# Feed-forward blocks: hidden-state tiles moved by 128 bytes in their partition

## The chip, the cores and the metric

One Trainium2 chip, one of its cores. The metric is the device time of one execution in microseconds, lower is better.

## The reference, cut to what matters

Two decoder layers over 512 tokens of width 1024, in float32. Each layer runs a SwiGLU feed-forward block, a token mixer (differential attention in layer 0, a pooling mixer in layer 1), cross-attention into 256 memory tokens, and a second feed-forward block; a layer norm follows each. The change touches the four feed-forward blocks:

```python
def swiglu_ffn(x, w_in, w_out):          # w_in: 1024 x 5632, w_out: 2816 x 1024
    h = x @ w_in
    g, u = jnp.split(h, 2, axis=-1)
    return (jax.nn.silu(g) * u) @ w_out
```

## The kernel before, in words

**Precision.** A float32 operand is split into a high part, rounded to the matmul engine's float32r type, and the remainder. `split` makes both, the high part on ScalarE (ACT), the low one on VectorE (DVE). `mm3` (lines 231 to 233) multiplies with three matmuls: high by high, high by low, low by high. In `mm3(out, w, x)` w is the stationary operand, loaded 128 columns at a time, and x the moving one, streamed through.

**A feed-forward block** (`ffn`) cuts the 2816 hidden units into eleven columns of 256.
- `up` computes one column: seven products of blocks of x and of w_in (a scheme of seven products in place of eight), each of 24 matmuls with 256 moving columns, summed in PSUM tiles named x, y and z. The weights (wh, wl) are stationary, x is moving: from xh and xl, or from sums of its blocks in xe. The first product of a column that goes by passes is recorded at line 773.
- `seven` forms the blocks and sums of h that the second matrix product needs, and splits them into the tiles ha and hb.
- `down` multiplies two columns of h by their rows of w_out, again in seven products, each of 12 matmuls with 512 moving columns, into px, py and pz. Here h (ha, hb) is stationary and the weights (wh, wl) are moving. DVE adds each result into the tokens X.
- `plain_down` does the last three columns without that scheme, into ps; there h stands in xe. For the first half of the output columns the weights stand in wh and wl, for the second half in hb and ha (line 983 on).

The order is written out by hand (`FFN_TURNS`): in the first turn three columns of `up` alone, then four turns in which products of two columns of `up` alternate with the products of one `down`, and `plain_down` at the end. One product of `up` or two (24 or 48 matmuls) stand between two blocks of `down`.

**Queues.** Weights come by DMA from the SP and POOL queues into ra, rc (for w_in) and b1 to b4 (for w_out), and are split into wh and wl just ahead of their product.

**Where the tiles lie.** A pool is a run of bytes in every partition; pools stack up in the order in which they are entered. `stage_pools` makes wh, wl, ra, rc, `phase_pool` the rest in the order of its arguments. Pads set the addresses modulo 512 bytes: `to_w` ahead of wh (64 bytes in this stage), and `to_x` (448 bytes) where a phase names `_x`. All tiles of the stage are whole multiples of 512 bytes. So, counted from the end of the tiles xh and xl, the weights stand at 64 modulo 512, and xe, hb, sp, ha, sr and hr at 0:

```python
APART, ROUND, LINE = {"ffn": 64, "da": 448, "pool": 64}, 512, 480
...
    def to_x(self, ctx):

        self.pad(ctx, ROUND - self.apart)
```

The pooling mixer and the cross-attention of layer 1 use the same 64 bytes; there the query projection (output xq) has the weights (wh, wl) stationary and xh, xl moving, with 512 columns.

Of the kernel before, what the change touches and what calls it, by code (L numbers as in the profile page):

```python
# [126 lines left out]
class Trunk:  # L127
# [49 lines left out]
    @contextmanager  # L177
    def phase_pool(self, gain, spare, **bufs):

        self.gain, self.spare, self.bufs, self.phase = gain, spare, bufs, {}
        with ExitStack() as ctx:
            for t in bufs:
                if t == "_x":
                    self.to_x(ctx)
                elif t == "_w":
                    self.to_w(ctx)
                else:
                    self.phase[t] = self.stage.get(t) or ctx.enter_context(self.pool(t))  # L190
            yield
# [1540 lines left out]
        return self.stage_pools(5, dict(raw=raw), order)  # L1732

    def ffn_phase(self, **more):
        bufs = dict(b1=1, b3=1, b2=1, b4=1, _x=0, xe=6, hb=4, sp=4, ha=4, sr=1, hr=3)
        return self.phase_pool(("hr", "sr"), "sp", **bufs, **more)

    def ffn_first(self, layer, ln):
# [84 lines left out]
```

## Time and profile before

| | |
|---|---|
| median of 3 runs | 1897.52 us (1895.87 to 1897.72) |
| profiled execution | 1899.25 us, its span 1897.5 us |
| granted TensorE clock | 0.999 |
| TensorE matmul busy | 1886.5 us (99%), 13120 matmuls |
| TensorE weight load busy | 1730.9 us (91%) |
| VectorE, ScalarE, GpSimd busy | 1540.9, 1000.8, 308.2 us |
| HBM read | 274.79 MB |

In rows of the profile PE is TensorE's matmul, PEld its weight load, DVE VectorE, ACT ScalarE, POOL GpSimd; L232 is line 232 of the kernel. A row of a group ends with its busy time, the mean duration in ns of one instruction, and the idle time ahead of them. A matmul's duration (some 0.28 us with 256 columns, 0.39 with 512) is longer than the distance from its start to the next one's, since matmuls are pipelined: how fast they follow each other is read from start times. In a row of the timeline the first number is the start and the second the duration in us, and of a tile's names the one ahead of the arrow is written. In a row of the chain the second number is the time that the instructions named there take on it.

### The profile page before, as it was taken

Reading aid. Unit: us, or ns where it says so; the run is one execution under the profiler, and the core shown is the slowest. Engines: PE = TensorE matmul, PEld = TensorE weight load, DVE = VectorE, ACT = ScalarE, POOL = GpSimd, SP = SyncE. Lnnn points to the kernel's source line nnn. Section 1 sums busy time; section 2 is a strip of 40 time slices with the busy share of each in tenths; the row PEclk is TensorE's granted clock in tenths of the full one; section 3 lists DMA queues with packets and bytes.
Section 4 is the critical chain, followed back from the end, with each engine's and each line's share of the span. In section 5 each row is a group of like instructions: output and inputs, shape, how many; then the busy total and the mean of one; then the engine's idle time right before and its main releaser. Section 6 shows DMA issues by size and latency. Waiting matters only on the chain.

```text
span 1897.5 us, 32589 instructions
## 1 busy us (share of the span) xinstructions
PE 1886.5 (99%) x13120; PEld 1730.9 (91%) x13120; DVE 1540.9 (81%) x2246; ACT 1000.8 (53%) x1542; POOL 308.2 (16%) x274
## 2 busy tenths in 40 slices
PE   9999999999999999999999999999999999999998
PEld 8999998888889988999998999999899889999996
DVE  7888989888876558889887988898786568998886
ACT  6555554566654435555554655555455436555552
POOL 3112120112110002221220311212120012211210
PEclk9999999999999999999999999999999999999999
DMA  9978772322235327987785687777464438867861
GB/s 254 215 178 178 171 141 85 103 69 75 91 112 178 112 70 181 195 177 168 144 188 168 118 179 181 168 166 162 157 172 146 142 69 180 173 159 178 185 129 53
DMA packets 250055, 283.20 MB, mean 149 GB/s; under 512 B 8752, under 2 KB 213040, under 8 KB 249904
## 3 DMA queue, kind: packets, MB, share of 16 engines
q0 software_dynamic: 94080, 94.38, 32.3%
q1 hardware_dynamic: 155824, 186.74, 30.2%
q8 instruction: 103, 1.69, 0.4%
q14 instruction: 48, 0.39, 0.1%
HBM read 274.79 MB, written 4.19 MB: 147 GB/s over the span
## 4 chain that ended last, share of the span: by engine, by line
PE 96%; DMA 2%; DVE 1%; ACT 0%; SPq 0%; issue 0%; POOL 0%; DVEq 0%; ACTq 0%
PE x L231 7%; PE x L232 7%; PE x L233 7%; PE ps L231 5%; PE ps L233 4%; PE ps L232 4%; PE z L231 4%; PE z L233 4%; PE z L232 4%; PE px L233 3%; PE px L231 3%; PE px L232 3%; PE x L773 3%; PE y L231 2%; PE y L232 2%; PE y L233 2%
## 5 line engine op out<-in xcount | busy, mean ns | idle before, releaser
L741 POOL DMA_DIRECT2D ra<-in_ffn_w_in_dram x132 | 170.7, 1307 | 977.6 <-DVE wl L748 960.4
L746 ACT CAST wh<-ra 128x1024 fp32r<-128x1024 f32 x176 | 184.9, 1053 | 197.8 <-PE x L232 63.8
L748 DVE TENSOR_TENSOR wl<-ra,wh 128x1024 fp32r<-128x1024 f32 x176 | 214.2, 1220 | 64.7 <-ACT wh L746 64.0
L231 PE MATMUL x<-xe,wh 128*128 128x256 f32 x704 | 195.0, 277 | 0.0
L232 PE MATMUL x<-xe,wh 128*128 128x256 f32 x704 | 194.8, 277 | 0.0
L233 PE MATMUL x<-xe,wl 128*128 128x256 f32 x704 | 194.8, 277 | 0.0
L746 ACT CAST wh<-rc 128x1024 fp32r<-128x1024 f32 x132 | 138.9, 1053 | 100.3 <-PE x L232 41.6
L143 ACT CAST wh<-b 128x1024 fp32r<-128x1024 f32 x112 | 117.8, 1052 | 134.8 <-PE x L232 62.2
L748 DVE TENSOR_TENSOR wl<-rc,wh 128x1024 fp32r<-128x1024 f32 x132 | 159.5, 1218 | 24.7 <-ACT wh L746 24.7
L144 DVE TENSOR_TENSOR wl<-b,wh 128x1024 fp32r<-128x1024 f32 x112 | 136.7, 1220 | 40.9 <-ACT wh L143 40.9
L231 PE MATMUL x<-xh,wh 128*128 128x256 f32 x536 | 148.7, 277 | 0.0
L232 PE MATMUL x<-xl,wh 128*128 128x256 f32 x536 | 148.4, 277 | 0.0
L233 PE MATMUL x<-xh,wl 128*128 128x256 f32 x536 | 148.4, 277 | 0.0
L231 PEld LDWEIGHTS x<-xe,wh 128*128 128x128 f32 x704 | 132.4, 188 | 1.3
L232 PEld LDWEIGHTS x<-xe,wh 128*128 128x128 f32 x704 | 132.3, 188 | 1.3
L233 PEld LDWEIGHTS x<-xe,wl 128*128 128x128 f32 x704 | 132.2, 188 | 0.0
L144 DVE TENSOR_TENSOR wl<-raw,wh 128x1024 fp32r<-128x1024 f32 x64 | 78.5, 1233 | 45.8 <-ACT wh L143 45.2
L231 PEld LDWEIGHTS x<-xh,wh 128*128 128x128 f32 x536 | 100.8, 188 | 0.7
L232 PEld LDWEIGHTS x<-xl,wh 128*128 128x128 f32 x536 | 100.8, 188 | 0.7
L233 PEld LDWEIGHTS x<-xh,wl 128*128 128x128 f32 x536 | 100.7, 188 | 0.0
L143 ACT CAST wh<-raw 128x1024 fp32r<-128x1024 f32 x64 | 66.4, 1049 | 62.5 <-PE xq L232 18.2
L231 PE MATMUL z<-xe,wh 128*128 128x256 f32 x352 | 97.5, 277 | 0.0
(445 smaller groups left out, 6239.9 us busy)
## 6 DMA issues: line engine op xcount, KB each, us to landing
ra<-in_ffn_w_in_dram POOLq DMA_DIRECT2D x132, 512.0 KB, 7.0
rc<-in_ffn_w_in_dram SPq DMA_DIRECT2D x88, 512.0 KB, 5.8
b<-in_ffn_w_out_dram SPq DMA_DIRECT2D x76, 512.0 KB, 5.0
ra<-in_ffn_w_in_dram SPq DMA_DIRECT2D x44, 512.0 KB, 4.7
rc<-in_ffn_w_in_dram POOLq DMA_DIRECT2D x44, 512.0 KB, 7.3
raw<-in_xa_wkv_dram SPq DMA_DIRECT2D x16, 1024.0 KB, 5.4
raw<-in_da_w_qkv_dram SPq DMA_DIRECT2D x24, 512.0 KB, 3.7
raw<-in_xa_wq_dram SPq DMA_DIRECT2D x8, 1024.0 KB, 5.2
```

Of the source, the lines that this page charges most:

```text
L143: self.nc.scalar.copy(hi, src),
L144: self.nc.vector.tensor_sub(lo, src, hi.bitcast(F32)),
L231: self.first_mm = mm(out, w[0], x[0], start=start, stop=False, skip_group_check=again)
L232: mm(out, w[0], x[1], start=False, stop=False, skip_group_check=again)
L233: self.last_mm = mm(out, w[1], x[0], start=False, stop=stop, skip_group_check=again)
L741: nc.gpsimd.dma_start(t, source(*block), accum_op=ALU.add)
L746: hi = nc.scalar.copy(v[0], raw)
L748: lo = nc.vector.tensor_sub(v[1], raw, v[0].bitcast(F32))
L773: self.last_mm = nc.tensor.matmul(ps[:, j], v[i][:, k, j * P : (j + 1) * P], x[l][:, k], start=n == i == l == 0, stop=n == 7 and i == 1, s ...
```

## The change

A pad of 128 bytes (twice 64) is entered between xe and hb. hb, sp, ha, sr and hr of the feed-forward blocks move up by 128 bytes: ha and hb stand at 128 modulo 512, 64 above the weights, where they stood at 0, 64 below. Nothing else is added or moved: the instructions and their order are the same.

```diff
@@ phase_pool @@
                 elif t == "_w":
                     self.to_w(ctx)
+                elif t == "_h":
+                    self.pad(ctx, 2 * self.apart)
                 else:
@@ ffn_phase @@
-        bufs = dict(b1=1, b3=1, b2=1, b4=1, _x=0, xe=6, hb=4, sp=4, ha=4, sr=1, hr=3)
+        bufs = dict(b1=1, b3=1, b2=1, b4=1, _x=0, xe=6, _h=0, hb=4, sp=4, ha=4, sr=1, hr=3)
```

## The prediction

> **What bounds the kernel now.** I read the page first: the share of each engine, the clock, and the chain that ended last. Then what the matmul engine waited for, and last the start times of matmuls, which say what the page's means can't.
>
> ```profile
> span 1897.5 us, 32589 instructions
> PE 1886.5 (99%) x13120; PEld 1730.9 (91%) x13120; DVE 1540.9 (81%) x2246; ACT 1000.8 (53%) x1542; POOL 308.2 (16%) x274
> PEclk9999999999999999999999999999999999999999
> PE 96%; DMA 2%; DVE 1%; ACT 0%; SPq 0%; issue 0%; POOL 0%; DVEq 0%; ACTq 0%
> ```
>
> The matmul engine is busy 99% of the span at the full granted clock in all 40 slices, and 96% of the chain is its own work. Its waits, in total:
>
> ```profile
> PE idle L138 <- DVE hb L595: 1.3, 1, 1.3
> PE ps L231 <- DVE X L380: 0.8, 1, 0.8
> PE y L773 <- ACT wh L746: 0.5, 1, 0.5
> ```
>
> The longest are 1.3, 0.8 and 0.5 us. So nothing that happens on another engine or in a transfer is worth anything here. What counts is how fast matmuls of one shape follow each other, and the change touches just that: the address of an operand.
>
> Define the offset of a matmul as the address of its stationary operand less that of its moving one, modulo 512 bytes. All tiles of the feed-forward stage are whole multiples of 512 bytes and all slices start on such multiples, so only the pads count: x (xh, xl, xe) stands at 0, the weights (wh, wl) at 64, and ha, hb at 0 now. In `up` weights are stationary and x moves: +64. In `down` h is stationary and weights move: -64. In the second half of `plain_down` h from xe is stationary and weights in hb and ha move: 0; in its first half weights in wh move: -64. In layer 1's cross-attention the query projection has weights at 64 stationary and x at 0 moving, 512 columns wide: +64, the offset that `down` is to get.
>
> Matmul starts from the timeline of TensorE, first row of a block and first row of what follows:
>
> ```profile
> 816.02 0.39 PE L231 MATMUL pz<-wh,hb 128*128 128x512 f32 x1
> ...
> 818.77 0.28 PE L231 MATMUL z<-xe,wh 128*128 128x256 f32 x1
> ```
>
> `down` (-64): 12 matmuls in 2.75 us, 229.2 ns each.
>
> ```profile
> 1451.86 0.39 PE L231 MATMUL xq<-xh,wh 128*128 128x512 f32 x1
> ...
> 1454.66 0.28 PE L231 MATMUL xs<-kv,q 128*128 128x256 f32 x1
> ```
>
> The query projection (+64): 12 in 2.80 us, 233.3 ns each.
>
> ```profile
> 1035.26 0.39 PE L231 MATMUL ps<-ha,xe 128*128 128x512 f32 x1
> ...
> 1040.70 0.40 PE L231 MATMUL ps<-wh,xe 128*128 128x512 f32 x1
> ```
>
> `plain_down` (0): 24 in 5.44 us, 226.7 ns each. Same engine, shape and type, three paces.
>
> ```profile
> 76.83 0.40 PE L231 MATMUL px<-wh,ha 128*128 128x512 f32 x1
> ...
> 79.63 0.28 PE L231 MATMUL y<-xh,wh 128*128 128x256 f32 x1
> ...
> 85.09 0.39 PE L231 MATMUL py<-wh,ha 128*128 128x512 f32 x1
> ```
>
> The very first `down` block, though at -64, also took 2.80 us, 233.3 ns each; the 48 matmuls of `up` behind it took 5.46 us, 113.8 ns each. Rows of 24 matmuls of `up`, from the chain:
>
> ```profile
> 71.34 2.83 PE x L773 x24
> 129.06 2.75 PE x L773 x24
> ...
> 794.32 2.72 PE x L773 x24
> ...
> 1059.12 2.83 PE x L773 x24
> ```
>
> At one offset (+64) `up` has two paces: 117.9 ns (71.34, ahead of the first `down` block, and 1059.12, right behind `plain_down`) and 113.3 ns (794.32). The row at 129.06, right behind a `down` block, is 114.6: a few longer distances, then the 113.3 of 794.32. So a pace depends on the offset and on what the matmuls ahead left behind.
>
> **The change part by part.** It adds one pool with one tile of 128 bytes a partition, and no instruction, transfer, wait or semaphore. It moves hb, sp, ha, sr and hr up by 128 bytes. ACT and DVE work on the moved tiles costs nothing as long as the waits above stay as they are; its cover is TensorE's 1886.5 busy us. A moved tile also lies differently over the tiles of the stages beside it, so a wait at a stage's border may shift; by the rows above I bound that by 0.8 us either way and take 0.
>
> First term, `down`: 4 groups of 7 products of 12 matmuls in each of 4 feed-forward blocks, 1344. The groups agree, each standing three times (L231, L232, L233):
>
> ```profile
> L233 PE MATMUL px<-wh,hb 128*128 128x512 f32 x192 | 75.5, 393 | 0.0
> L233 PE MATMUL pz<-wh,hb 128*128 128x512 f32 x128 | 50.4, 394 | 0.0
> L233 PE MATMUL px<-wh,ha 128*128 128x512 f32 x64 | 25.2, 394 | 0.0
> L233 PE MATMUL py<-wh,ha 128*128 128x512 f32 x64 | 25.2, 394 | 0.0
> L233 PE MATMUL ps<-hb,xe 128*128 128x512 f32 x60 | 23.5, 392 | 0.0
> L233 PE MATMUL ps<-ha,xe 128*128 128x512 f32 x30 | 11.7, 390 | 0.0
> ```
>
> (192 + 128 + 64 + 64) x 3 = 1344. They go from -64 to +64. Bounds from the nearest rows: 226.7 (the best pace of this shape) and 233.3 ns (the worst). I take 233.3, since the one block shown at just this offset and width has it: 112 blocks x (2.80 - 2.75) = +5.6 us. Lower end: 1344 x (226.7 - 229.2) = -3.4 us.
>
> On this a rule of the Trainium skill speaks. "TensorE: Matmul & The Clock Gate", section "Step-by-step: what each phase is for", says that TensorE reads SBUF through two independent ports, one for the streaming operand and one for the weight load, so that loading the next weights takes nothing from the running matmul. By it the offset could not matter, and this term would be 0. The trace does not agree: 226.7, 229.2 and 233.3 ns for one shape.
>
> Second term, `plain_down`: (60 + 30) x 3 = 270 matmuls whose moving weights stand in hb and ha go from offset 0 to -128, which no row shows. Bounds: 0 (they stay at 226.7) and 270 x 6.6 ns = +1.8 us. I take +0.5, nearer the lower end, since the blocks at 0 already begin slower than they go on.
>
> Third term, `up`, whose own offset stays: 11 columns of 7 products of 24 matmuls; the last 8 run between `down` blocks, less the 48 ahead of the first: 8 x 168 - 48 = 1296 in each feed-forward block, 5184 in all. They now take 113.8 ns. If `down` leaves them as it does now, 0. Bounds: 5184 x (113.3 - 113.8) = -2.6 us (113.3 from the start) and 5184 x (117.9 - 113.8) = +21 us (slow throughout). I take 0, because the one `down` block that did run at 233.3 ns (76.83) was followed by `up` at 113.8.
>
> Sum: 5.6 + 0.5 + 0 = +6.1 us. The profiled execution took 1899.25 us, 1.73 above the median of the runs shown, its span 1897.5; against it the sum is 1905.35, against the median 1897.52 it is 1903.6.
>
> **The rivals.** (1) *`up` falls to its slow pace for good.* For it: 1059.12, where `up` behind a block at 226.7 ns ran slow over all 24 matmuls, and 71.34. It seems that today's -64 blocks are what brings `up` to the fast pace: the rows behind them read 2.75 (129.06). Against it: the block at 76.83. Price: 5.6 + 0.5 + 21 = +27 us, 1925. It decides if the first 24 of `up` behind each `down` block take 2.83 us.
>
> (2) *Faster: `down` goes without conflict.* `up` itself, in its fast pace, runs at +64 and at 113.3 ns for 256 columns, which is half of 226.7: nothing is lost at this offset. If a wider matmul entered from that pace keeps the same distance between its two reads, `down` comes to 226.7 ns: -3.4 us, and with the longer starts of `up` gone -6.0: 1891.5 to 1894. For it: each `down` block is entered from `up`, and the query projection, which I went by, is entered from other work. Against it: the query projection keeps 233.3 to its twelfth matmul. It decides where the pace falls below 229.2.
>
> (3) *No change, 1897.5.* The pace hangs on what ran before and hardly on the sign of the offset (76.83 shows 233.3 at -64): 229.2 stays, and the sum is within 1.5 us of 0. Against it: the query projection has 233.3 with `xs`, not `up`, ahead of it, and every later `down` block 229.2. The rule of the Trainium skill on the two ports, named above, would give the same time.
>
> **How the numbers follow.** The forecast (`down` at 233.3, `up` as now) has 0.42, rival 1 0.33, rival 2 0.12, rival 3 0.13. About 0.2%, 3.8 us, is what a measurement of this kernel can tell from no change. The forecast's own range is 1900.5 to 1907: -2.6 to +1.8 for the open ends of terms two and three, 0.8 for the borders. The whole range leaves out rival 2 alone: 1896 to 1926. Slower by over 0.2%: 0.42 less a little for its lower edge, and rival 1: 0.73. Within: rival 3 and those edges, 0.17. Faster: most of rival 2, 0.10.
>
> **What the changed profile would show.** Right: blocks px, py, pz of 12 in 2.80 us instead of 2.75, the chain's rows of 24 behind them at 2.72 to 2.75, the same waits of TensorE, DVE, ACT and DMA totals as before. The second term shows in the blocks of ps from ha, now 226.7. Wrong: rows of 24 at 2.83 behind every `down` block (rival 1), blocks of 12 in 2.72 (rival 2), or a new wait of TensorE of more than 1 us.

## The result and the profile after

The changed kernel takes 1915.40 us (median of 5, 1915.09 to 1918.47) where the kernel before takes 1897.72 beside it: a ratio of 1.0098, 95% interval 1.0084 to 1.0111, so 17.7 us or 1% slower. The forecast was 1903.6.

The page of the changed kernel, first the span, the engines and the clock, then the chain. The change adds two lines ahead of `mm3`, so L231 to L233 of before are L233 to L235 here, and L773 is L775.

```profile
span 1913.3 us, 32589 instructions
PE 1902.2 (99%) x13120; PEld 1740.8 (91%) x13120; DVE 1545.1 (81%) x2246; ACT 1002.5 (52%) x1542; POOL 308.3 (16%) x274
PEclk9999999999999999999999999999999999999999
PE 98%; DMA 1%; SPq 0%; ACT 0%; DVE 0%; issue 0%; DVEq 0%; ACTq 0%
```

The same 13120 matmuls in the same order at the same clock, and 15.7 us more of busy TensorE for 15.8 us more of span. What TensorE waited for (total, times, longest):

```profile
PE idle L138 <- DVE hb L597: 1.2, 1, 1.2
PE x L775 <- ACT wh L748: 0.6, 2, 0.3
PE ps L233 <- DVE X L382: 0.5, 1, 0.5
```

These and four smaller ones sum to 3.3 us, as the waits of before do. The time lies in how fast matmuls follow each other, and the durations of the groups hardly tell it:

```profile
L235 PE MATMUL px<-wh,hb 128*128 128x512 f32 x192 | 75.9, 395 | 0.0
L235 PE MATMUL px<-wh,ha 128*128 128x512 f32 x64 | 25.3, 396 | 0.0
L235 PE MATMUL ps<-ha,xe 128*128 128x512 f32 x30 | 11.8, 394 | 0.0
```

Against the same rows of before (L233 there) these are 2, 2 and 4 ns longer, while the distance from start to start grew by about 4 in each. The timeline of TensorE shows that: the first row of each block of `down` (px) and of `up` (x), the kernel before ahead of the changed one.

```profile
109.73 0.39 PE L231 MATMUL px<-wh,hb 128*128 128x512 f32 x1
112.48 0.28 PE L231 MATMUL x<-xe,wh 128*128 128x256 f32 x1
117.94 0.39 PE L231 MATMUL px<-wh,hb 128*128 128x512 f32 x1
120.69 0.28 PE L231 MATMUL x<-xh,wh 128*128 128x256 f32 x1
126.16 0.39 PE L231 MATMUL px<-wh,hb 128*128 128x512 f32 x1
```

```profile
109.63 0.39 PE L233 MATMUL px<-wh,hb 128*128 128x512 f32 x1
112.42 0.28 PE L233 MATMUL x<-xe,wh 128*128 128x256 f32 x1
118.08 0.39 PE L233 MATMUL px<-wh,hb 128*128 128x512 f32 x1
120.88 0.28 PE L233 MATMUL x<-xh,wh 128*128 128x256 f32 x1
126.34 0.39 PE L233 MATMUL px<-wh,hb 128*128 128x512 f32 x1
129.13 0.28 PE L775 MATMUL x<-xh,wh 128*128 128x256 f32 x1
```

Before: 12 matmuls of `down` in 2.75 us and 48 of `up` in 5.46 or 5.47, again and again. After: `down` 2.79 and 2.80 in turn, `up` 5.66 (112.42 to 118.08) and 5.46 (120.88 to 126.34) in turn. `up`, whose own operands did not move, loses 0.2 us behind every second block of `down`. The chain's rows of 24 say the same for column starts:

```profile
129.29 2.83 PE x L775 x24
187.86 2.74 PE x L775 x24
246.24 2.83 PE x L775 x24
```

Over all blocks, from the differences of successive start times (gaps left out; matmuls of other shapes changed by less than 0.5 us each):

| | matmuls | before, ns | after, ns | us |
|---|---|---|---|---|
| `down` | 1344 | 229.0 | 232.8 | +5.1 |
| `up` from the first `down` on | 5184 | 113.8 | 116.0 | +11.4 |
| `plain_down`, weights in hb and ha | 270 | 228.5 | 232.45 | +1.1 |
| `up` ahead of the first `down` blocks | 2208 | 114.45 | 113.8 | -1.4 |

The four give +16.2, the span +15.8; the gaps left out make up the difference. The last row stands ahead of all moved matmuls: in the profiled execution of before the first feed-forward block ran `up` at 117.9 ns until its first `down` block (71.34 in the prediction's rows), in that of the kernel after at 113.3. Without this row the sum is +17.6, close to the 17.7 between the medians; at which pace the other executions began is not on record.

### The profile page after: what moved, and what is told of

It reads as the page before. It is cut to its first block, busy times and chain, and to the rows that moved or that the text cites. A ratio compares the mean times of both kernels' runs of the same rounds, so it can differ in the third digit from the quotient of the medians.

```text
span 1913.3 us, 32589 instructions
## 1 busy us (share of the span) xinstructions
PE 1902.2 (99%) x13120; PEld 1740.8 (91%) x13120; DVE 1545.1 (81%) x2246; ACT 1002.5 (52%) x1542; POOL 308.3 (16%) x274
## 4 chain that ended last, share of the span: by engine, by line
PE 98%; DMA 1%; SPq 0%; ACT 0%; DVE 0%; issue 0%; DVEq 0%; ACTq 0%
PE x L235 7%; PE x L233 7%; PE x L234 7%; PE ps L233 5%; PE ps L235 5%; PE ps L234 5%; PE z L235 4%; PE z L233 4%; PE z L234 4%; PE px L233 3%; PE px L235 3%; PE px L234 3%; PE x L775 3%; PE y L235 2%; PE y L233 2%; PE y L234 2%
## 5 line engine op out<-in xcount | busy, mean ns | idle before, releaser
L235 PE MATMUL x<-xe,wl 128*128 128x256 f32 x704 | 195.7, 278 | 0.0
L233 PE MATMUL x<-xe,wh 128*128 128x256 f32 x704 | 195.7, 278 | 0.0
L143 ACT CAST wh<-b 128x1024 fp32r<-128x1024 f32 x112 | 117.8, 1052 | 145.5 <-PE x L234 62.5
L233 PE MATMUL x<-xh,wh 128*128 128x256 f32 x536 | 149.4, 279 | 0.0
L235 PE MATMUL x<-xh,wl 128*128 128x256 f32 x536 | 149.2, 278 | 0.0
L233 PEld LDWEIGHTS x<-xe,wh 128*128 128x128 f32 x704 | 132.2, 188 | 1.4
L235 PEld LDWEIGHTS x<-xe,wl 128*128 128x128 f32 x704 | 132.1, 188 | 0.0
L233 PEld LDWEIGHTS x<-xh,wh 128*128 128x128 f32 x536 | 100.6, 188 | 0.7
L235 PEld LDWEIGHTS x<-xh,wl 128*128 128x128 f32 x536 | 100.6, 188 | 0.0
L235 PE MATMUL z<-xe,wl 128*128 128x256 f32 x352 | 97.9, 278 | 0.0
```

What stands on the lines that cost most here:

```text
L143: self.nc.scalar.copy(hi, src),
L233: self.first_mm = mm(out, w[0], x[0], start=start, stop=False, skip_group_check=again)
L235: self.last_mm = mm(out, w[1], x[0], start=False, stop=stop, skip_group_check=again)
```

## The experiments

All timed runs stand beside runs of the kernel before on the same chip, at about 1898 us. In each only the places of the moved tiles differ (ha, hb and, with them, sp, sr, hr); the weights and x stay. Edits are shown against the changed kernel. "Above" and "below" are counted from the weights, modulo 512. One `down` is seven blocks in this order: px and py from ha, then two of pz and three of px from hb.

**Theory A**: a `down` block at +64, entered from `up` at 113.3 ns, leaves `up` at 117.8; entered at 117.8, it leaves 113.3. At -64 it leaves 113.3. The next two runs mix both offsets. First, ha alone moved:

```diff
-xe=6, _h=0, hb=4, sp=4, ha=4, sr=1, hr=3
+xe=6, hb=4, sp=4, _h=0, ha=4, sr=1, hr=3
```

> Only ha (with sr, hr) stands 64 above the weights; hb is back at 64 below. Theory A (a down block at +64 flips the pace of `up` behind it, 113.3 to 117.9 ns and back; one at -64 leaves or brings 113.3): the ha blocks come in pairs (px, py) and each pair is entered at 113.3, so the 48 of `up` behind px<-ha take 5.66 us and those behind py<-ha 5.46; behind all five hb blocks 5.46. Down: px<-ha 232.4 ns, py<-ha 233.3, hb blocks 229.0. Time: down +1.5, up 16 x 0.19 = +3.1, plain_down +0.5: about +5 us against the kernel before, 1903. Rival B (every second down block leaves `up` at 117.9, whatever its address): `up` goes 5.66, 5.46 in turn behind hb blocks too, +11 us, 1908. Rival C (no flip, +64 simply leaves 117.9): both blocks of each pair are followed by 5.66, +6 us and over, 1905.

1904.55 us, ratio 1.0034 (1.0022 to 1.0046). Block starts in its timeline:

```profile
76.81 0.39 PE L233 MATMUL px<-wh,ha 128*128 128x512 f32 x1
79.60 0.28 PE L233 MATMUL y<-xh,wh 128*128 128x256 f32 x1
85.26 0.39 PE L233 MATMUL py<-wh,ha 128*128 128x512 f32 x1
88.06 0.28 PE L233 MATMUL z<-xh,wh 128*128 128x256 f32 x1
93.52 0.39 PE L233 MATMUL pz<-wh,hb 128*128 128x512 f32 x1
...
96.26 0.28 PE L233 MATMUL z<-xe,wh 128*128 128x256 f32 x1
101.73 0.39 PE L233 MATMUL pz<-wh,hb 128*128 128x512 f32 x1
```

5.66 behind px<-ha (79.60 to 85.26), 5.46 behind py<-ha, 5.47 behind pz<-hb: theory A's row of numbers, and it holds in all 16 pairs and all 68 hb blocks with `up` behind them. B and C are out: the address decides, and the pace at entry. The time alone, 6.5 us more than before, would not have told A from C; the starts do. Next, hb alone:

```diff
-xe=6, _h=0, hb=4, sp=4, ha=4, sr=1, hr=3
+xe=6, sp=4, ha=4, sr=1, hr=3, _h=0, hb=4
```

> Only hb stands 64 above the weights (its pool is entered last, so that ha, sp, sr, hr are back at 64 below). Theory A: five hb blocks in a row, entered at 113.3, are followed by 48 of `up` in 5.66, 5.46, 5.66, 5.46, 5.66 us; the px<-ha block behind is at -64, is entered at 117.9, takes 2.80 us itself and brings 113.3 back; py<-ha 2.75. Time: down +4.2, up 48 x 0.19 = +9.2, plain_down +1: about +14.5 us, 1912. Rival A' (a block at -64 does not bring 113.3 back, it only keeps what it finds): px<-ha and py<-ha are followed by 5.66 too, +17 us, 1915. Rival C (no flip): all five followed by 5.66, +20 us.

1916.05 us, 1.0093 (1.0079 to 1.0106), 18 us where 14.5 was expected. The starts in its trace give just that 14.5 (`down` +4.2, `up` +9.4, `plain_down` +0.9); where the rest lies is not shown, and the four runs spread from 1913.71 to 1917.34. The hb blocks flip `up` 39 times from 113.3 and 29 times back, as A says. Of 13 ha blocks (-64) entered at 117.8, 11 brought 113.3 back; these two did not:

```profile
78.00 0.40 PE L233 MATMUL px<-wh,ha 128*128 128x512 f32 x1
80.76 0.28 PE L233 MATMUL y<-xh,wh 128*128 128x256 f32 x1
...
86.42 0.40 PE L233 MATMUL py<-wh,ha 128*128 128x512 f32 x1
89.18 0.28 PE L233 MATMUL z<-xh,wh 128*128 128x256 f32 x1
...
94.84 0.39 PE L233 MATMUL pz<-wh,hb 128*128 128x512 f32 x1
```

Two blocks of 2.76 us (not 2.75, nor 2.80), and `up` at 5.66 behind both. The first of the two follows the `up` at the kernel's head; but in the kernel before, too, the head ran at 117.8, and there the block at -64 took 2.80 and brought 113.3 (76.83 in the prediction's rows). So 117.8 ns is more than one state, told apart by what follows: from one, a block at -64 takes 2.80 and brings 113.3; from another it takes 2.76 and keeps 117.8. Theory A is too simple there.

**Other offsets.** h level with the weights:

```diff
-self.pad(ctx, 2 * self.apart)
+self.pad(ctx, self.apart)
```

> h level with the weights (offset 0 in `down`). Theory A (as in plain_down of the kernel before: 512-wide matmuls at offset 0 go at 226.7 ns and leave `up` at 117.9): down 112 x 12 at about 227.2 ns = -2.4 us, `up` at 117.9 behind every down block, 5184 x 4.0 ns = +20.7, plain_down (now -64) +0.6: about +19 us, 1917. Rival D (a down block with no conflict leaves `up` as it found it, at 113.3): down -2.4, up -2.6, about -4.5 us, 1893.

1918.00 us, 1.0102 (1.0089 to 1.0116): theory A.

```profile
803.20 0.39 PE L233 MATMUL px<-wh,ha 128*128 128x512 f32 x1
805.93 0.28 PE L233 MATMUL y<-xh,wh 128*128 128x256 f32 x1
811.59 0.39 PE L233 MATMUL py<-wh,ha 128*128 128x512 f32 x1
814.30 0.28 PE L233 MATMUL z<-xh,wh 128*128 128x256 f32 x1
819.96 0.39 PE L233 MATMUL pz<-wh,hb 128*128 128x512 f32 x1
```

`down` comes down to 226.7 ns (811.59 to 814.30, 2.71 as printed), the best of all places tried, and `up` goes to 5.66 behind every block. The changed matmuls gain 2.9 us, their neighbours lose 20.5 (5184 x (117.78 - 113.83)).

The pad in the following kernels is a number in the place of `2 * self.apart`: 192, 256, 32, 224, 96 and 160 bytes.

> h 128 above the weights (offset +128 in `down`, 320 in plain_down's second half). Theory A says only that pace and state follow the offset; nothing shown has +128 with 512 columns, and plain_down's second half at -128 in the changed kernel took 232.5 ns in a pattern of 228 to 241. If +128 is like -128: down +4.7 us, `up` unknown, 0 to +21, so 1902 to 1923. Rival E (only operands 64 apart disturb each other): down at 226.7, -3.1 us, `up` 113.3 throughout, 1892.

1913.00 us, 1.0079 (1.0066 to 1.0091). `down` 231.4 ns, `up` flipping in every pair; rival E is out. The distances inside a block, 228, 230, 232, 241, were those that `plain_down` at -128 had shown, which led to theory F.

> h 192 above the weights. In the run with h 128 above, `down` at +128 showed the same distances (228, 230, 232, 241) as plain_down at -128 in the changed kernel, and plain_down at 320, which is +64 modulo 256, showed 231 and 236 in turn as `down` at +64. Theory F: only the offset modulo 256 counts. Then +192 is -64 and plain_down's 256 is 0: `down` 229.0 ns, `up` 113.9 behind every block, time as before, 1898 within 2 us. Rival G (the period is 512, and +192 is one more offset with a conflict): `down` 231 to 233, `up` flipping as in the runs at +64 and +128, 1913.

1898.70 us, 1.0000 (0.9991 to 1.0009): F. The blocks are those of the kernel before:

```profile
806.57 0.39 PE L233 MATMUL py<-wh,ha 128*128 128x512 f32 x1
809.32 0.28 PE L233 MATMUL z<-xh,wh 128*128 128x256 f32 x1
814.78 0.39 PE L233 MATMUL pz<-wh,hb 128*128 128x512 f32 x1
```

2.75 and 5.46. `plain_down`, now at -256, takes 228.5 ns, as at 0 in the kernel before. So the period is 256 bytes, for both things: the pace and what is left behind. +128 and -128 are the same place. No run moved the weights, but rows with other addresses and the same offset agree: at +64 the query projection (233.3) and `down` of the changed kernel (232.8), at 0 `plain_down` of the kernel before (226.7 at its best) and level `down` (226.8). That speaks for the difference of the two addresses as what counts.

> h 32 below the weights, between the kernel before (64 below: `down` 229.0, `up` 113.9) and level (226.7, `up` 117.9). Theory H (steps of 64 bytes are what counts, and half a step acts like one of its neighbours): either 1898 or 1917, with just their rows. Rival I (the pace follows the offset in between): `down` 227 to 229 and `up` at 113.9 or better for both, 1893 to 1897: faster than before.

1924.87 us, 1.0135 (1.0118 to 1.0153). Both H and I were wrong: it is neither like a neighbour nor between them. `down` takes 233.2 and `up` 117.8 behind every block:

```profile
814.76 0.39 PE L233 MATMUL py<-wh,ha 128*128 128x512 f32 x1
817.56 0.28 PE L233 MATMUL z<-xh,wh 128*128 128x256 f32 x1
823.21 0.39 PE L233 MATMUL pz<-wh,hb 128*128 128x512 f32 x1
```

> h 160 above the weights, which modulo 256 is 96 below. By theory F with H it acts like +128 (231.3 ns, `up` flipping, 1913) or like -64 (1898). By rival I it lies between: `down` 229 to 231.3, `up` 113.9 or flipping, 1898 to 1913. Under the 512 period nothing is known of it.

1906.58 us, 1.0040 (1.0027 to 1.0053): within I's span, but not by its rows, since `down` at 233.1 is above both neighbours; `up` stays at 113.9.

> h 32 above the weights, between level (226.7, `up` 117.9 throughout, 1918) and +64 (232.8, `up` flipping, 1915). Theory H: just one of these two. Rival I: `down` about 230, `up` between half and all at 117.9, 1916 to 1921. Both expect slower than before by about 1%; faster than 1905 would speak against all of it.

1903.33 us, 1.0023 (1.0013 to 1.0032): below the 1905 that was to speak against both H and I. `down` 232.8, and `up` at 113.6 behind every block, better than before:

```profile
806.95 0.39 PE L233 MATMUL py<-wh,ha 128*128 128x512 f32 x1
809.74 0.28 PE L233 MATMUL z<-xh,wh 128*128 128x256 f32 x1
815.20 0.39 PE L233 MATMUL pz<-wh,hb 128*128 128x512 f32 x1
```

This run is the forecast's world, though at another offset: `down` of the changed kernel's pace (+5.1), `up` left alone (5184 x (113.59 - 113.83) = -1.2), `plain_down` +1.3, in all +5.2, and +5.0 measured. It isolates the first term, and shows that the pace of a block and what it leaves to `up` are two things.

> h 96 above the weights, the last step of 32 bytes modulo 256 that no run has. The pace of `down` and the state it leaves to `up` have not gone together so far: +32 and +160 gave 232.8 and 233.0 ns with `up` at 113.6 and 114.0, +64 and +128 gave 232.8 and 231.3 with `up` flipping, -32 gave 233.2 with `up` at 117.8. Theory J (the two are separate; odd multiples of 32 take about 233 ns, and `up` is one of the three kinds seen): `down` 233, so 1902 to 1904 (`up` fast), 1913 to 1915 (flipping) or 1925 (117.8). Rival I (in between its neighbours +64 and +128): `down` 232, `up` flipping, 1914.

1923.62 us, 1.0134 (1.0116 to 1.0153): theory J with `up` at 117.8 throughout (J left open which kind it would be); I is out. The last run asks again what a block at -64 does with 117.8, with ha level and hb at -64:

```diff
-xe=6, _h=0, hb=4, sp=4, ha=4, sr=1, hr=3
+xe=6, hb=4, sp=4, _h=0, ha=4, sr=1, hr=3
...
-self.pad(ctx, 2 * self.apart)
+self.pad(ctx, self.apart)
```

> ha level with the weights (offset 0), hb 64 below as before. It asks whether a block at -64 brings `up` back from the pace that a block at 0 leaves. Theory A: px<-ha 228 and py<-ha 226.7 ns, `up` behind both 5.65 us per 48; the next block, pz<-hb at -64, is entered at 117.8, takes 2.80 us, and `up` behind it and behind the other hb blocks takes 5.46. Time: 16 pairs x (2 x 0.19 + 0.05 - 0.04) = +6.2 us, 1904. Rival A' (a block at -64 keeps what it finds, as two of 13 did with hb alone moved): hb blocks at 230.6 or so and `up` at 5.65 behind all, about +21 us, 1919.

1918.12 us, 1.0105 (1.0087 to 1.0123): A failed, A' holds.

```profile
819.06 0.40 PE L233 MATMUL pz<-wh,hb 128*128 128x512 f32 x1
821.83 0.28 PE L233 MATMUL z<-xe,wh 128*128 128x256 f32 x1
...
827.48 0.40 PE L233 MATMUL pz<-wh,hb 128*128 128x512 f32 x1
```

pz<-hb, at -64 as before, takes 2.77 and `up` behind it 5.65, and so do all 68 hb blocks that have `up` behind them. The 117.8 that a level block leaves is the kind that -64 keeps. "A block at -64 brings 113.3" is therefore not a rule.

The offsets of `down` in steps of 32 bytes, modulo 256, with the mean distance of `down` and of the 5184 `up` behind. The kind says what `up` settles to behind a block: "113.3 kept" is `up` entered and left at 113.3 after a few longer distances, "in turn" is 117.8 and 113.3 alternating:

| offset | `down`, ns | `up`, ns | kind | us |
|---|---|---|---|---|
| -64 (before; +192) | 229.0 | 113.8 | 113.3 kept | 1898 (1898.70) |
| -32 | 233.2 | 117.8 | 117.8 behind all | 1924.87 |
| 0 | 226.8 | 117.8 | 117.8 behind all | 1918.00 |
| +32 | 232.8 | 113.6 | 113.3 kept | 1903.33 |
| +64 (after) | 232.8 | 116.0 | in turn | 1915.40 |
| +96 | 232.8 | 117.8 | 117.8 behind all | 1923.62 |
| +128 | 231.4 | 115.8 | in turn | 1913.00 |
| +160 | 233.1 | 113.9 | 113.3 kept | 1906.58 |

None of these offsets beats the kernel before; the one at +192 equals it.

## Why the prediction failed in one term

The forecast was 1903.6, within 1900.5 to 1907, and the measured 1915.40 lies 8.4 us above that range (whose own terms give 1900.2 to 1906.2). The whole range, 1896 to 1926, holds the result only because it also spans rival 1; that is width and luck, since no case of the prediction had `up` alternate between its two paces, as the runs showed. Of the 17.6 us that the starts show, the forecast's terms explain 6.2.

**What bounds the kernel**: right. The waits' total is the same, so is the clock, and 15.7 of 15.8 us are TensorE's own.

**First term, `down` at 233.3 ns, +5.6**: right. 232.8, +5.1. The query projection was a good row for it; blocks entered at 113.3 ns begin with 227 and 229 and so come to 232.4, the others to 233.3. Rival 2, which took `up`'s 113.3 at +64 as half of 226.7, is refuted: at +64 256 columns go at 113.3 ns, and 512 columns at 232.8, not at twice 113.3. Rival 3 (the offset hardly counts) fell too. So did the reading of the rule of the Trainium skill ("TensorE: Matmul & The Clock Gate", "Step-by-step: what each phase is for") by which two ports make the offset free: from the same instructions, places of h gave 1898 to 1925 us.

**Second term, `plain_down`, +0.5 of 0 to 1.8**: +1.1, inside its bounds, mis-sized. At -128 the 512-wide matmul takes 232.45 ns. From the first of these rows to the second lie 24 matmuls with weights in ha, hb and ha:

```profile
1042.42 0.39 PE L233 MATMUL ps<-ha,xe 128*128 128x512 f32 x1
...
1047.99 0.40 PE L233 MATMUL ps<-wh,xe 128*128 128x512 f32 x1
```

5.57 us against 5.44 for the same 24 of before (1035.26 to 1040.70). I had no row at -128 and leaned to the lower end for no good reason.

**Third term, `up`, 0**: this is the step that failed, by 11.4 us. I took 0 because the one `down` block of before that ran at 233.3 ns (76.83) was followed by `up` at 113.8. That block was entered from `up` at 117.9, and at -64. What it showed was one half of a rule: a block that finds 117.8 can leave 113.3. How a block at 233 that finds 113.3 leaves `up`, which is the usual case, no row of before showed at this offset. What the runs showed instead: at +64 such a block leaves 117.8, the next one takes it back, and so over half of `up` pays: 60 of the 108 groups of 48 run at 117.85, 60 x 48 x (117.85 - 113.85) = +11.5. Most pairs of `down` blocks have 48 matmuls of `up` between them, but once in each feed-forward block it is six products, 144 matmuls, counted here as three groups. All of them pay, since the pace lasts until the next block:

```profile
246.07 0.28 PE L775 MATMUL x<-xh,wh 128*128 128x256 f32 x1
...
263.04 0.39 PE L233 MATMUL px<-wh,ha 128*128 128x512 f32 x1
```

144 matmuls in 16.97 us, 117.8 ns each.

**Rival 1** named the place, `up` left at its slow pace behind `down`, with 0.33, but as all or nothing: "every `down` block" was its condition, +21 its price. The truth lay near half, 10 us below its 1925, and in no case of the list. Its guess that the -64 blocks are what brings `up` to the fast pace is not the whole either: in the trace of before, `up` ran slow at 1059.12, and behind eight transposes, with no `down` block between, it went on from 1062.58 and settled at 113.3. What would have given it: treating the two paces of `up` as states, asking for each state what a block does to it, and a case for "flips".

## What to carry to other kernels

- Where TensorE is the bound and weight loads run beside matmuls, the place of the stationary against the moving operand modulo 256 bytes is a parameter worth 1.4% here, in steps of 32 bytes. Sweep it; values between two known ones need not lie between them in time (-32 is the worst place tried, between the two best paces of `down`).
- Judge such a change by the distance from start to start, in the block that it touches and in the block behind it. At offset 0 the touched matmuls were the fastest of all, and the kernel was 20 us slower by what they left to their neighbours.
- One block is no evidence on a state. Look for rows of each entry state before you set a term to 0, and let a rival have the case that the states alternate.

## What the runs showed of the hardware

- In blocks of 12, a 512-wide float32r matmul followed the one ahead in 226.7 to 233.3 ns on average. The offset sets it, with period 256 bytes, and to a lesser degree the pace that the block was entered at: at -64 a block took 2.75 us entered at 113.3, and 2.76 to 2.80 entered at 117.8; at +64 2.79 and 2.80.
- 256-wide ones have paces of 113.3 and 117.8 ns at one offset (+64), and keep the one they have through 144 matmuls. What goes ahead sets it, and 117.8 comes in at least two kinds that a block at -64 tells apart (2.80 us and back to 113.3, or 2.76 and kept).
- The kernel's head ran at either pace with the same instructions and the same offsets: its first 552 matmuls of `up` took 117.15 ns each in the profiled execution of before and 114.0 in that of the changed kernel, 1.7 us (gaps left out). In the profiled executions of hb alone, of h level and of h 128 above it was slow too, in the other eight fast at the first `down` block.
- What in the chip makes the period, what the states are, and what sets the pace of the head, stays open. That the load of the next weights and the stream meet in memory fits an effect that hangs on the two addresses together, but no run here shows it; no run changed the timing at a block's entry alone.
